# Two-layer decoder trunk: attention norm weights folded into the rows of the output weights, rotary tables made earlier

## The chip, the cores and the metric

The kernel runs on one core of a Trainium2 chip. The metric is the device time of one execution in microseconds, as the median of several runs. The core has five engines that run beside each other, each with its own queue of instructions, which it takes in order: TensorE (PE in the profile; its weight loads are PEld), VectorE (DVE), ScalarE (ACT), GpSimd (POOL), and SyncE (SP), which here only issues DMA transfers (SPq). They wait for one another by semaphores.

## The reference

A decoder trunk of two layers on 256 tokens of width 1024. Layer 0 mixes tokens by gated linear attention (GLA, 4 heads, key width 128, value width 256, chunks of 64), layer 1 by a block-sparse softmax attention with partial rotary embedding; each is followed by a normalisation and a SwiGLU feed-forward. What the change touches:

```python
def gla_mixer(x, w_in, w_gk, b_gk, norm_g, w_out):
    q, k, v, g, gk_low = split_cols(x @ w_in, GLA_COLS)
    ...
    o = from_heads(rms_norm(o.astype(x.dtype), norm_g)) * jax.nn.silu(g)
    return o @ w_out

def partial_rope(x, positions):
    ang = positions.astype(jnp.float32)[:, None, :, None] * inv_freq
    cos, sin = jnp.cos(ang), jnp.sin(ang)
    ...
```

`norm_g` has 256 entries, one for each value feature of a head; the four heads share it. `partial_rope` is used in layer 1 alone, and its tables depend on the positions only.

## The kernel before

All products are done in three matmuls of rounded fp32: a matrix is split into a high part (rounded) and a low part (what is left), and high x high, low x high and high x low are added in PSUM. For weights this is `split`: one DMA of 512 KB into a raw tile (name with `r`), a cast on ScalarE (name with `h`), a subtraction on VectorE (name with `l`). The 256 tokens are two tiles of 128, `t` = 0 and 1.

The order of the first attention as written: `v` block 0, the gate `gk` and from it `z`, `la`, `cum` and three exponentials `em`, `ee`, `ep`; the keys (`wk`, giving `ka`, `ke`, and by copies on GpSimd `kb` and `kx`), the queries (`wq`, giving `qd` in two halves), the scores `sc` and `scx`, `v` block 1 (`wv1`). Then for each token tile the output `o`, the sums of squares `ss`, the two halves of the gate `sg` (weights `wg0`, `wg1`; matmuls, silu on ScalarE, and a multiplication by `normg` on GpSimd), `og` = `o` x `ss` x `sg` on VectorE, its transposes `trg` on TensorE and the split of these into `ogT`. `out_proj` multiplies `ogT` by eight row blocks `wo0` to `wo7` of the output weights into `y`, and adds and normalises. After it `rope_tables` makes the cosine and sine tables of layer 1: three small loads (`rcol`, `cmask`, `posb`), eighteen small VectorE instructions on 32x256 tiles (`ang`, `kk`, `rr`), two sines on ScalarE. The feed-forward (`fg`, `fu`, `A`, `X`, `d`) follows.

No order of instructions is written out. `Plan.op` records each operation with its engine, an assumed duration, what it reads and writes; `Plan.emit` then simulates the engines with these durations and at each step takes the operation that can start first, by order of recording where two can start at once, and before that those marked urgent. The instructions go to the queues in the order so found. Weights and intermediates take 41 slots of SBUF in turn; a load is issued when its slot is free. The planner may therefore put work of a later stage into an earlier one: in the queue of VectorE the rotary instructions stand between the `og` of tile 1 before the change.

Each load on SP also waits for the transfer eight loads back.

Of the kernel before, what the change touches and what calls it, by code (L numbers as in the profile page):

```python
# [10 lines left out]
I32 = mybir.dt.int32  # L11
AF = mybir.ActivationFunctionType
ALU = mybir.AluOpType
# [176 lines left out]
def kernel(ctx, tc, x, positions, gla_w_in, gla_w_gk, gla_b_gk, gla_norm_g, gla_w_out,  # L190
# [30 lines left out]
    normg = fixed("normg", (P, GLA_DV))  # L221
# [29 lines left out]
    def split(name, parts, zero=False):  # L251
# [9 lines left out]
        act(1024, lambda: nc.scalar.copy(hi.r, raw.f), [raw], [hi])  # L261
        dve(1024, lambda: nc.vector.tensor_tensor(out=lo.r, in0=raw.f, in1=hi.f, op=ALU.subtract), [raw, hi], [lo])
# [19 lines left out]
    def w_row(name, w, k):  # L282
        return split(name, lambda raw: [(raw, w[k * P:(k + 1) * P, :])])
# [133 lines left out]
    def out_proj(aT, w, xo, gb, dstT, keep):  # L417
        ws = [w_row(f"wo{k}", w, k) for k in range(KT)]
# [379 lines left out]
    dma(lambda: nc.sync.dma_start(normg.f, gla_norm_g[0:1, :].broadcast_to([P, GLA_DV])), 128, [], [normg])  # L798
# [25 lines left out]

    wv1 = load_cols("wv1", w0, V0 + 512)
# [6 lines left out]
    def g_block(blk, t, ws):  # L832
        ps = pl.buf("acc", f"g{blk}{t}")
        act_block(ps, T0, ws, t)
        sl = slice(512 * blk, 512 * blk + 512)
        act(512, lambda: nc.scalar.activation(sg[t].f[:, sl], ps.f, AF.Silu), [ps], [(sg[t], blk)], table="silu")

        def fg():
            v3 = sg[t].f[:, sl].rearrange("p (j c) -> p j c", j=2)
            nc.gpsimd.tensor_tensor(out=v3, in0=v3, in1=normg.f.unsqueeze(1).broadcast_to([P, 2, GLA_DV]), op=ALU.mult)  # L840
        gps(512, fg, [(sg[t], blk), normg], [(sg[t], blk)])
# [62 lines left out]
    xs = out_proj(ogT, gla_w_out[0], xs, gb, T1, x32)  # L904


    posb, ang, kk_, rr_ = S_("posb"), S_("ang"), S_("kk"), S_("rr")

    def q32(b):
        return b.f[0:ROPE, 0:S]  # L910

    def rope_tables():
        dma(lambda: nc.sync.dma_start(rcol.f, c_f32[:, 2 * P:2 * P + 2]), 4, [], [rcol])
        dma(lambda: nc.sync.dma_start(cmask.f, c_f32[:, P:2 * P]), 64, [], [cmask])
        dma(lambda: nc.sync.dma_start(q32(posb).bitcast(I32), positions[0:1, :].broadcast_to([ROPE, S])), 32,
            [], [posb])

        def f0():
            nc.vector.tensor_copy(q32(ang), q32(posb).bitcast(I32))
            nc.vector.tensor_scalar_mul(q32(ang), q32(ang), rcol.f[0:ROPE, 0:1])  # L920
        dve(512, f0, [posb, rcol], [ang])
        for which, off in ((0, 0.25), (1, 0.0)):
            def f1(off=off, which=which):
                k_, r_, a_ = q32(kk_), q32(rr_), q32(ang)
                nc.vector.tensor_scalar(out=k_, in0=a_, scalar1=1.0 / TWO_PI, scalar2=off, op0=ALU.mult, op1=ALU.add)
                nc.vector.tensor_scalar_add(k_, k_, MAGIC)
                nc.vector.tensor_scalar_add(k_, k_, -MAGIC)
                nc.vector.scalar_tensor_tensor(out=r_, in0=k_, scalar=-C1, in1=a_, op0=ALU.mult, op1=ALU.add)

            def f2(which=which):  # L930
                k_, r_ = q32(kk_), q32(rr_)
                nc.vector.scalar_tensor_tensor(out=r_, in0=k_, scalar=-C2, in1=r_, op0=ALU.mult, op1=ALU.add)
                nc.vector.scalar_tensor_tensor(out=r_, in0=k_, scalar=-C3, in1=r_, op0=ALU.mult, op1=ALU.add)
                if which == 0:
                    nc.vector.tensor_scalar_add(r_, r_, math.pi / 2.0)
# [169 lines left out]
```

## Time and profile before

| | |
|---|---|
| median of 3 runs | 593.11 us (593.08 to 593.64) |
| profiled execution | 594.05 us; its span, first to last instruction, 592.1 us |
| TensorE busy | 578.4 us, 98% of the span |
| VectorE busy | 491.1 us, 83% |
| ScalarE busy | 327.4 us, 55% |
| GpSimd busy | 23.2 us, 4% |
| TensorE's share of the chain that ended last | 86% (VectorE 9%) |
| mean granted clock of TensorE | 0.993 |

Busy shares are means over stages. The waits of an engine say where it stood still and for whom; the timeline then gives the instructions around one wait, with the idle time ahead of an instruction and what ended it in brackets. The profile also has, for any stretch, the share of TensorE's full clock that the chip granted.

### The profile page before, as it was taken

To read this page: it belongs to the slowest core of one execution; us is meant where nothing else is said; L and a number is where in the kernel's file an instruction comes from. 1 tells how busy PE (TensorE), PEld (TensorE's weight loads), DVE (VectorE), ACT (ScalarE), POOL (GpSimd) and SP (SyncE) were. 2 spreads that over 40 slices of the span, in tenths; PEclk is the share of its full clock that TensorE was granted. 3 is DMA by queue.
4 is the path that set the end of the run, shared out by engine and by line. 5 is a ranking of instruction groups with operands and counts; after the bars stand their busy time and mean duration, and the time that the engine had idled before them with its cause. 6 is when DMAs were issued, how large, how long until landed. Compare 5 with 4: busy or idle time off the path is not lost.

```text
span 592.1 us, 8004 instructions
## 1 busy us (share of the span) xinstructions
PE 578.4 (98%) x3030; PEld 494.0 (83%) x3030; DVE 491.1 (83%) x609; ACT 327.4 (55%) x434; POOL 23.2 (4%) x27
## 2 busy tenths in 40 slices
PE   8999998999999999999999999999999999999994
PEld 7899886888888788889888999888888888888883
DVE  5889268889999986999696589988999998689626
ACT  4794455246767634786264356644685775359310
POOL 1022210000000000000000000000000000000001
PEclk9999998999999999999999999999999999999998
DMA  8984285254656737688365435726457484559101
GB/s 285 380 283 150 68 280 184 54 195 163 230 176 201 258 111 215 200 296 277 114 214 181 150 134 192 234 73 213 143 193 234 143 277 150 167 176 311 58 1 71
DMA packets 51880, 110.04 MB, mean 186 GB/s; under 512 B 4689, under 2 KB 9329, under 8 KB 51842
## 3 DMA queue, kind: packets, MB, share of 16 engines
q1 hardware_dynamic: 51842, 109.53, 56.6%
q8 instruction: 24, 0.39, 0.3%
q14 instruction: 14, 0.11, 0.1%
HBM read 108.47 MB, written 1.05 MB: 185 GB/s over the span
## 4 chain that ended last, share of the span: by engine, by line
PE 86%; DVE 9%; issue 2%; DMA 2%; ACT 0%; SPq 0%; DVEq 0%
PE fy L291 6%; PE fy L289 6%; PE fy L290 6%; PE pa L542 3%; PE pa L539 3%; PE pa L541 3%; PE pg L289 3%; PE v L291 3%; PE pg L291 3%; PE v L289 2%; PE v L290 2%; PE pu L289 2%; PE pu L291 2%; PE pg L290 2%; PE pu L290 2%; PE tr L304 2%
## 5 line engine op out<-in xcount | busy, mean ns | idle before, releaser
L559 DVE TENSOR_TENSOR A<-A,X 128x1024 f32<-128x1024 f32 x36 | 43.2, 1218 | 3.3 <-DMA X<-in_ffn_w_gu 3.2
L313 ACT CAST xT<-tr 128x512 fp32r<-128x512 f32 x16 | 9.3, 592 | 40.4 <-PE tr L304 40.4
L360 POOL TENSOR_TENSOR st<-st,mhalf 128x1 f32<-128x1 f32 x8 | 7.5, 944 | 483.6 <-DVE st L358 483.6
L317 DVE TENSOR_TENSOR xT<-tr,xT 128x512 fp32r<-128x512 f32 x16 | 10.7, 686 | 7.7 <-ACT xT L313 5.6
L348 DVE SCALAR_TENSOR_TENSOR r<-xn,fy 128x512 f32<-128x512 f32 x8 | 5.5, 685 | 10.9 <-PE fy L291 10.9
L559 DVE TENSOR_TENSOR X<-X,X 128x1024 f32<-128x1024 f32 x12 | 14.3, 1216 | 0.0
L313 ACT CAST hT3h<-tr 128x512 fp32r<-128x512 f32 x4 | 2.4, 588 | 18.0 <-PE tr L304 18.0
L352 DVE BATCH_NORM_STATS2 st<-r 128x6 f32<-128x512 f32 x16 | 11.1, 693 | 0.5
L370 DVE SCALAR_TENSOR_TENSOR xn<-r,st,lnb 128x512 f32<-128x512 f32 x16 | 11.3, 745 | 0.0
L366 DVE SCALAR_TENSOR_TENSOR r<-r,st,lng 128x512 f32<-128x512 f32 x16 | 11.2, 743 | 0.0
L497 ACT CAST D0h<-A 128x1024 fp32r<-128x1024 f32 x6 | 6.3, 1054 | 8.0 <-DVE A L559 7.9
L497 ACT CAST B0h<-A 128x1024 fp32r<-128x1024 f32 x6 | 6.3, 1052 | 5.8 <-DVE A L559 5.8
L518 DVE TENSOR_TENSOR sil<-pu,sil 128x512 f32<-128x512 f32 x8 | 5.5, 685 | 4.7 <-PE pu L291 4.7
L497 ACT CAST F0h<-X 128x1024 fp32r<-128x1024 f32 x6 | 6.3, 1051 | 5.4 <-DVE X L559 5.4
L497 ACT CAST A0h<-A 128x1024 fp32r<-128x1024 f32 x6 | 6.3, 1046 | 5.0 <-DMA A<-in_ffn_w_gu 5.0
L498 DVE TENSOR_TENSOR C1l<-X,C1h 128x1024 fp32r<-128x1024 f32 x6 | 7.3, 1220 | 1.7 <-ACT C1h L497 1.7
L968 ACT ACTIVATE mk<-mk 128x512 f32<-128x512 f32 x4 | 2.4, 599 | 11.5 <-PE mk L291 11.5
L317 DVE TENSOR_TENSOR hT3l<-tr,hT3h 128x512 fp32r<-128x512 f32 x4 | 2.8, 690 | 7.0 <-ACT hT3h L313 7.0
L498 DVE TENSOR_TENSOR G0l<-A,G0h 128x1024 fp32r<-128x1024 f32 x6 | 7.3, 1217 | 1.5 <-ACT G0h L497 1.5
L304 PE MATMUL tr<-ident,e 128*128 128x128 f32 x48 | 7.3, 274 | 1.1 <-DVE e L586 1.1
L304 PEld LDWEIGHTS tr<-ident,e 128*128 128x128 f32 x48 | 5.7, 140 | 3.0 <-issue 1.8
L497 ACT CAST G0h<-A 128x1024 fp32r<-128x1024 f32 x6 | 6.3, 1048 | 3.2 <-DVE A L559 3.2
(1098 smaller groups left out, 2292.3 us busy)
## 6 DMA issues: line engine op xcount, KB each, us to landing
X<-in_ffn_w_gu SPq DMA_DIRECT2D x36, 512.0 KB, 4.6
A<-in_ffn_w_gu SPq DMA_DIRECT2D x12, 512.0 KB, 4.6
lng<-in_ln_g SPq DMA_DIRECT2D x4, 512.0 KB, 3.9
lnb<-in_ln_b SPq DMA_DIRECT2D x4, 512.0 KB, 5.5
x<-in_x SPq DMA_DIRECT2D x4, 256.0 KB, 4.5
fg00r<-in_ffn_w_gu SPq DMA_DIRECT2D x2, 512.0 KB, 6.1
fg01r<-in_ffn_w_gu SPq DMA_DIRECT2D x2, 512.0 KB, 6.4
fg02r<-in_ffn_w_gu SPq DMA_DIRECT2D x2, 512.0 KB, 5.8
```

What stands on the lines that cost most here:

```text
L289: nc.tensor.matmul(ps, lh, rh, start=start, stop=False)
L290: nc.tensor.matmul(ps, ll, rh, start=False, stop=False)
L291: nc.tensor.matmul(ps, lh, rl, start=False, stop=stop)
L304: nc.tensor.transpose(ps.f[:, j * P:(j + 1) * P], src.f[:, k * P:(k + 1) * P], ident.f)
L313: nc.scalar.copy(view(0), ps.f.rearrange("p (k c) -> p k c", k=4))
L317: nc.vector.tensor_tensor(out=l, in0=ps.f.rearrange("p (k c) -> p k c", k=4), in1=h.bitcast(F32), op=ALU.subtract)
L497: act(1024, lambda: nc.scalar.copy(hi.r, raw.f), [raw], [hi])
L498: dve(1024, lambda: nc.vector.tensor_tensor(out=lo.r, in0=raw.f, in1=hi.f, op=ALU.subtract), [raw, hi], [lo])
L539: nc.tensor.matmul(ps.f, sh, wh.r[:, cs], start=first and q == 0 and j == 0, stop=False, skip_group_check=True)
L541: nc.tensor.matmul(ps.f, sl_, wh.r[:, cs], start=False, stop=False, skip_group_check=True)
L542: nc.tensor.matmul(ps.f, sh, wl.r[:, cs], start=False, stop=last_ and q == 1 and j == 1, skip_group_check=True)
L559: dve(1024, lambda q=q, other=other: nc.vector.tensor_tensor(out=raws[q].f, in0=raws[q].f, in1=other.f, op=ALU.add), [raws[q], other], [ra ...
```

## The change

The multiplication of the gate by `normg` on GpSimd goes. Since `norm_g` multiplies the columns of what `out_proj` multiplies by the output weights, it can as well multiply the rows of these weights: row `p` of block `k` by `norm_g[(k % 2) * 128 + p]`. `normg` becomes a tile of 128x2, loaded by 256 pieces of 4 bytes in place of 128 rows of 1 KB, and `split` gets a scale: the cast becomes an activation (copy) with a scale for each row, the subtraction a `scalar_tensor_tensor` that multiplies the raw weights by the same scale and subtracts the high part. This holds for the eight `wo` of the first attention; the second attention's stay as they are.

`rope_tables` is recorded after the scores, ahead of `v` block 1, instead of ahead of the feed-forward; its text is the same. The planner does the rest.

```diff
--- before.py
+++ after.py
@@ -218,7 +218,7 @@
     cmask = fixed("cmask", (P, P))
     imask = fixed("imask", (P, P), I32)
     rcol = fixed("rcol", (P, 2))
-    normg = fixed("normg", (P, GLA_DV))
+    normg = fixed("normg", (P, GLA_DV // P))
     wgk = fixed("wgk", (GLA_RANK + 1, 512))
     gkT = fixed("gkT", (GLA_RANK + 1, S))
     rope = fixed("rope", (ROPE, 2, S))
@@ -248,7 +248,8 @@
         return pl.op("POOL", 1.3, fn, reads, writes, extra=8.0, **kw)
 
 
-    def split(name, parts, zero=False):
+    def split(name, parts, zero=False, scale=None):
+
         raw, hi, lo = S_(name + "r"), S_(name + "h", True), S_(name + "l", True)
         if zero:
             gps(500, lambda: nc.gpsimd.memset(raw.f, 0.0), [], [raw])
@@ -258,8 +259,13 @@
             for dst, src in parts(raw.f):
                 nc.sync.dma_start(dst, src)
         dma(load, kb, [], [raw])
-        act(1024, lambda: nc.scalar.copy(hi.r, raw.f), [raw], [hi])
-        dve(1024, lambda: nc.vector.tensor_tensor(out=lo.r, in0=raw.f, in1=hi.f, op=ALU.subtract), [raw, hi], [lo])
+        if scale is None:
+            act(1024, lambda: nc.scalar.copy(hi.r, raw.f), [raw], [hi])
+            dve(1024, lambda: nc.vector.tensor_tensor(out=lo.r, in0=raw.f, in1=hi.f, op=ALU.subtract), [raw, hi], [lo])
+        else:
+            act(1024, lambda: nc.scalar.activation(hi.r, raw.f, AF.Copy, scale=scale[1]), [raw, scale[0]], [hi])
+            dve(1024, lambda: nc.vector.scalar_tensor_tensor(out=lo.r, in0=raw.f, scalar=scale[1], in1=hi.f,
+                                                             op0=ALU.mult, op1=ALU.subtract), [raw, hi, scale[0]], [lo])
         return hi, lo
 
     def split2(name, w, k0, c0):
@@ -279,8 +285,8 @@
         src = w[k0 * P:(k0 + nk) * P, c0:c0 + n].rearrange("(k p) c -> p k c", p=P)
         return split(name, lambda raw: [(raw.rearrange("p (k c) -> p k c", k=nk), src)])
 
-    def w_row(name, w, k):
-        return split(name, lambda raw: [(raw, w[k * P:(k + 1) * P, :])])
+    def w_row(name, w, k, scale=None):
+        return split(name, lambda raw: [(raw, w[k * P:(k + 1) * P, :])], scale=scale)
 
     def load_cols(name, w, c0):
         return [w_kcols(f"{name}{i}", w, 2 * i, 2, c0, 512) for i in range(KT // 2)]
@@ -414,8 +420,8 @@
         sl = slice(512 * blk, 512 * blk + 512)
         act(512, lambda: nc.scalar.copy(vt[t].f[:, sl], ps.f), [ps], [(vt[t], blk)])
 
-    def out_proj(aT, w, xo, gb, dstT, keep):
-        ws = [w_row(f"wo{k}", w, k) for k in range(KT)]
+    def out_proj(aT, w, xo, gb, dstT, keep, scale=None):
+        ws = [w_row(f"wo{k}", w, k, scale and scale(k)) for k in range(KT)]
         xn = []
         for t in range(2):
             y = [pl.buf("acc", f"y{t}{hf}") for hf in range(2)]
@@ -795,7 +801,8 @@
     gps(350, lambda: nc.gpsimd.tensor_copy(kxv()[:, 1, :, 0:CHUNK], ch(qd, 2)), [qd], [(kx, 3)])
 
     dma(lambda: nc.sync.dma_start(imask.f, c_i32), 64, [], [imask])
-    dma(lambda: nc.sync.dma_start(normg.f, gla_norm_g[0:1, :].broadcast_to([P, GLA_DV])), 128, [], [normg])
+    dma(lambda: nc.sync.dma_start(normg.f, gla_norm_g[0].rearrange("(c p) -> p c", p=P),
+                                  ), 8, [], [normg])
     scs = [S_("sc0"), S_("scx")]
 
     def scv(i):
@@ -822,6 +829,45 @@
     pe(4 * 512, fscx, [kx], [psx])
     act(512, lambda: nc.scalar.copy(scv(2), psx.f.rearrange("p (h c) -> p h c", h=GLA_H)), [psx], [(scs[1], 0)])
 
+
+    posb, ang, kk_, rr_ = S_("posb"), S_("ang"), S_("kk"), S_("rr")
+
+    def q32(b):
+        return b.f[0:ROPE, 0:S]
+
+    def rope_tables():
+        dma(lambda: nc.sync.dma_start(rcol.f, c_f32[:, 2 * P:2 * P + 2]), 4, [], [rcol])
+        dma(lambda: nc.sync.dma_start(cmask.f, c_f32[:, P:2 * P]), 64, [], [cmask])
+        dma(lambda: nc.sync.dma_start(q32(posb).bitcast(I32), positions[0:1, :].broadcast_to([ROPE, S])), 32,
+            [], [posb])
+
+        def f0():
+            nc.vector.tensor_copy(q32(ang), q32(posb).bitcast(I32))
+            nc.vector.tensor_scalar_mul(q32(ang), q32(ang), rcol.f[0:ROPE, 0:1])
+        dve(512, f0, [posb, rcol], [ang])
+        for which, off in ((0, 0.25), (1, 0.0)):
+            def f1(off=off, which=which):
+                k_, r_, a_ = q32(kk_), q32(rr_), q32(ang)
+                nc.vector.tensor_scalar(out=k_, in0=a_, scalar1=1.0 / TWO_PI, scalar2=off, op0=ALU.mult, op1=ALU.add)
+                nc.vector.tensor_scalar_add(k_, k_, MAGIC)
+                nc.vector.tensor_scalar_add(k_, k_, -MAGIC)
+                nc.vector.scalar_tensor_tensor(out=r_, in0=k_, scalar=-C1, in1=a_, op0=ALU.mult, op1=ALU.add)
+
+            def f2(which=which):
+                k_, r_ = q32(kk_), q32(rr_)
+                nc.vector.scalar_tensor_tensor(out=r_, in0=k_, scalar=-C2, in1=r_, op0=ALU.mult, op1=ALU.add)
+                nc.vector.scalar_tensor_tensor(out=r_, in0=k_, scalar=-C3, in1=r_, op0=ALU.mult, op1=ALU.add)
+                if which == 0:
+                    nc.vector.tensor_scalar_add(r_, r_, math.pi / 2.0)
+                nc.vector.tensor_scalar(out=r_, in0=r_, scalar1=SIN_MAX, scalar2=-SIN_MAX, op0=ALU.min, op1=ALU.max)
+            dve(900, f1, [ang], [kk_, rr_])
+            dve(900, f2, [kk_, rr_], [rr_])
+            act(256, lambda which=which: nc.scalar.activation(rope.f[:, which, :], q32(rr_), AF.Sin), [rr_],
+                [(rope, which)], table="silu")
+        dve(256, lambda: nc.vector.tensor_scalar_mul(rope.f[:, 1, :], rope.f[:, 1, :], rcol.f[0:ROPE, 1:2]),
+            [(rope, 1), rcol], [(rope, 1)])
+
+    rope_tables()
     wv1 = load_cols("wv1", w0, V0 + 512)
     v_block(1, 0, T0, wv1, v_sb)
 
@@ -834,11 +880,6 @@
         act_block(ps, T0, ws, t)
         sl = slice(512 * blk, 512 * blk + 512)
         act(512, lambda: nc.scalar.activation(sg[t].f[:, sl], ps.f, AF.Silu), [ps], [(sg[t], blk)], table="silu")
-
-        def fg():
-            v3 = sg[t].f[:, sl].rearrange("p (j c) -> p j c", j=2)
-            nc.gpsimd.tensor_tensor(out=v3, in0=v3, in1=normg.f.unsqueeze(1).broadcast_to([P, 2, GLA_DV]), op=ALU.mult)
-        gps(512, fg, [(sg[t], blk), normg], [(sg[t], blk)])
 
     wgs = [load_cols("wg0", w0, G0), load_cols("wg1", w0, G0 + 512)]
     for t in range(2):
@@ -901,49 +942,10 @@
     gb = load_ln(0, 0)
     T1 = new_xT("xT1")
     x32 = [S_("x32a"), S_("x32b")]
-    xs = out_proj(ogT, gla_w_out[0], xs, gb, T1, x32)
-
-
...
     gb = load_ln(0, 1)
     T2 = new_xT("xT2")
-    rope_tables()
     xs = ffn(0, xs, T1, gb, T2, False, x32)
 
 
```

(The removed copy of `rope_tables` is left out; it reads as the added one.)

Where it lands. VectorE at the end of the first attention, before (`og` is that of tile 1, `ss` its scale by the sums of squares; `kk` and `rr` are rotary):

```order
L936 TENSOR_SCALAR rr_894<-rr_894 32x256
L262 TENSOR_TENSOR fg00l_932<-fg00r_885,fg00h_907 128x1024
L925 TENSOR_SCALAR kk_893<-ang_889 32x256
L926 TENSOR_SCALAR kk_893<-kk_893 32x256
L927 TENSOR_SCALAR kk_893<-kk_893 32x256
L928 SCALAR_TENSOR_TENSOR rr_894<-kk_893,ang_889 32x256
L262 TENSOR_TENSOR fg01l_953<-fg01r_905,fg01h_922 128x1024
L896 TENSOR_TENSOR ogT_763<-trg_943,ogT_762 128x512
L879 SCALAR_TENSOR_TENSOR og_0_909<-o_0_822,ss_829,sg_0_887 128x256 x2
L932 SCALAR_TENSOR_TENSOR rr_894<-kk_893,rr_894 32x256
L933 SCALAR_TENSOR_TENSOR rr_894<-kk_893,rr_894 32x256
L936 TENSOR_SCALAR rr_894<-rr_894 32x256
```

and after:

```order
L920 SCALAR_TENSOR_TENSOR og_0_912<-o_0_833,ss_852,sg_0_910 128x256 x2
L264 TENSOR_TENSOR fg00l_931<-fg00r_893,fg00h_923 128x1024
L264 TENSOR_TENSOR fg01l_943<-fg01r_908,fg01h_935 128x1024
L264 TENSOR_TENSOR fg02l_959<-fg02r_920,fg02h_947 128x1024
L920 SCALAR_TENSOR_TENSOR og_0_912<-o_0_845,ss_852,sg_0_910 128x256
L937 TENSOR_TENSOR ogT_787<-trg_949,ogT_786 128x512
L920 SCALAR_TENSOR_TENSOR og_0_912<-o_0_845,ss_852,sg_0_910 128x256
L264 TENSOR_TENSOR fg03l_981<-fg03r_933,fg03h_965 128x1024
```

The rotary instructions are gone from between the parts of `og`; the splits of `fg01` and `fg02` have come ahead of the second half of `og`, which is now taken in two steps.

ScalarE at the same place, before:

```order
L836 ACTIVATE sg_0_887<-g_0_837 128x512
L261 CAST fg00h_907<-fg00r_885 128x1024
L261 CAST fg01h_922<-fg01r_905 128x1024
L939 ACTIVATE rope<-rr_894 32x256
L261 CAST fg02h_935<-fg02r_930 128x1024
L836 ACTIVATE sg_0_887<-g_0_878 128x512
L892 CAST ogT_762<-trg_943 128x512
```

and after:

```order
L882 ACTIVATE sg_0_910<-g_0_860 128x512
L263 CAST fg00h_923<-fg00r_893 128x1024
L263 CAST fg01h_935<-fg01r_908 128x1024
L263 CAST fg02h_947<-fg02r_920 128x1024
L882 ACTIVATE sg_0_910<-g_0_901 128x512
L933 CAST ogT_786<-trg_949 128x512
```

The sine ahead of `fg02h` is gone; the second silu still stands behind the cast of `fg02h`.

VectorE in the front of the first attention, before (`z`, `cum`, `ee` lead to the exponentials):

```order
L733 TENSOR_SCALAR z_311<-pre_308 128x512
L262 TENSOR_TENSOR wq2l_333<-wq2r_242,wq2h_299 128x1024
L742 TENSOR_TENSOR z_311<-z_311,la_313 128x1024
L744 SCALAR_TENSOR_TENSOR cum_395<-smask_90,z_311 128x1024
L753 TENSOR_TENSOR ee_411<-cum_395 128x1024
L262 TENSOR_TENSOR wq3l_429<-wq3r_273,wq3h_376 128x1024
L262 TENSOR_TENSOR wv10l_444<-wv10r_296,wv10h_393 128x1024
```

and after:

```order
L264 TENSOR_TENSOR wq2l_333<-wq2r_242,wq2h_301 128x1024
L845 CAST ang_349<-posb_298 32x256
L846 TENSOR_SCALAR ang_349<-ang_349,rcol 32x256
L851 TENSOR_SCALAR kk_352<-ang_349 32x256
L852 TENSOR_SCALAR kk_352<-kk_352 32x256
L853 TENSOR_SCALAR kk_352<-kk_352 32x256
L854 SCALAR_TENSOR_TENSOR rr_353<-kk_352,ang_349 32x256
L858 SCALAR_TENSOR_TENSOR rr_353<-kk_352,rr_353 32x256
L859 SCALAR_TENSOR_TENSOR rr_353<-kk_352,rr_353 32x256
L861 TENSOR_SCALAR rr_353<-rr_353 32x256
L862 TENSOR_SCALAR rr_353<-rr_353 32x256
L748 TENSOR_TENSOR z_313<-z_313,la_315 128x1024
```

Ten rotary instructions stand between the split of `wq2` and `z`. The second pass stands further on, among `ka`, `ke` and `kx`, and on ScalarE a table load and a sine stand ahead of the exponentials, a second pair behind the casts of `wv1`; the casts of `wv10` and `wv11` have moved behind the exponentials. On SP `rcol`, `cmask` and `posb` are issued right behind `normg`, ahead of `wv10r`. On TensorE two things move: the six matmuls of `wv11` for `v` of tile 0 go ahead of the scores, and the second `trg` of tile 0 goes ahead by six matmuls.

## Rows read from the trace of the kernel before

**Rows 1.** Waits of TensorE over the whole span: us in total, times, longest.
```profile
PE trg L888 <- DVE og L879: 2.7, 1, 2.7
...
PE tr L304 <- DVE e L586: 1.1, 1, 1.1
```

**Rows 2.** Timeline of TensorE: start, length, engine, line, operation, idle before.
```profile
92.14 0.60 PE L888 MATMUL trg<-ident,og 128*128 128x128 f32 x4
...
93.98 0.39 PE L289 MATMUL y<-wo2h,ogT 128*128 128x512 f32 x1
...
98.92 1.08 PE L888 MATMUL trg<-ident,og 128*128 128x128 f32 x4 [2.67 <-DVE og L879]
...
102.30 0.40 PE L289 MATMUL y<-wo7h,ogT 128*128 128x512 f32 x1
```

**Rows 3.** Stretches: busy time of each engine with instructions, PEclk, DMA share, GB/s.
```profile
60.00:80.00 20.00, 20.00 (x94) 16.65 (x93) 8.23 (x12) 10.70 (x21) 3.60 (x3) 1.00 0.39 133
...
98.90:102.30 3.40, 3.38 (x10) 2.84 (x11) 3.02 (x6) 1.83 (x3) 0.00 (x0) 0.51 0.35 69
199.70:204.70 5.00, 4.99 (x24) 4.23 (x25) 5.00 (x6) 4.29 (x5) 0.00 (x0) 1.00 0.73 220
```

**Rows 4.** Timelines of ScalarE, GpSimd and VectorE ahead of that `trg`.
```profile
93.14 0.42 ACT L939 ACTIVATE rope<-rr 32x256 f32<-32x256 f32 x1 [1.76 <-DVE rr L936]
93.47 1.03 ACT L261 CAST fg02h<-fg02r 128x1024 fp32r<-128x1024 f32 x1
94.41 0.59 ACT L836 ACTIVATE sg<-g 128x512 f32<-128x512 f32 x1
...
95.07 1.30 POOL L840 TENSOR_TENSOR sg<-sg,normg 128x512 f32<-128x512 f32 x1 [6.14 <-ACT sg L836]
...
95.19 1.46 DVE L928 SCALAR_TENSOR_TENSOR rr<-kk,ang 32x256 f32<-32x256 f32 x1
...
97.71 0.67 DVE L896 TENSOR_TENSOR ogT<-trg,ogT 128x512 fp32r<-128x512 f32 x1
98.31 0.85 DVE L879 SCALAR_TENSOR_TENSOR og<-o,ss,sg 128x256 f32<-128x256 f32 x2
```

**Rows 5.** Lines of VectorE, 60 to 100 us: busy us, mean ns, idle before.
```profile
L879 DVE SCALAR_TENSOR_TENSOR og<-o,ss,sg 128x256 f32<-128x256 f32 x8 | 3.5, 472 | 5.3 <-POOL sg L840 5.3
```

**Rows 6.** The load of fg02r, by its tile: issue on SP, and landing.
```profile
L259 SPq DMA_DIRECT2D fg02r<-in_ffn_w_gu x1: 368/368/368, 86.7 to 86.7; - x1
...
DMA to landing us min/median/max: 5.0/5.0/5.0
```

**Rows 7.** Timeline of ScalarE, 28 to 32 us: a table load.
```profile
29.60 1.28 ACT L741 ACT_TABLE_LOAD   x1
30.89 1.06 ACT L741 ACTIVATE la<-la 128x1024 f32<-128x1024 f32 x1
```

**Rows 8.** Timeline of VectorE: front of the attention, and the first rotary pass.
```profile
31.98 1.23 DVE L742 TENSOR_TENSOR z<-z,la 128x1024 f32<-128x1024 f32 x1 [3.00 <-ACT la L741]
...
43.12 1.41 DVE L262 TENSOR_TENSOR wv12l<-wv12r,wv12h 128x1024 fp32r<-128x1024 f32 x1
...
50.00 0.68 DVE L773 SCALAR_TENSOR_TENSOR qd<-gq,ep 128x512 f32<-128x512 f32 x1
...
87.76 1.32 DVE L919 CAST ang<-posb 32x256 f32<-32x256 int32 x1 [2.37 <-DMA posb<-in_positions]
89.11 0.34 DVE L920 TENSOR_SCALAR ang<-ang,rcol 32x256 f32<-32x256 f32 x1
...
93.04 1.20 DVE L262 TENSOR_TENSOR fg00l<-fg00r,fg00h 128x1024 fp32r<-128x1024 f32 x1
```

**Rows 9.** The load of wv10r, by its tile: issue on SP, and landing.
```profile
L259 SPq DMA_DIRECT2D wv10r<-in_gla_w_in x1: 379/379/379, 18.0 to 18.0; - x1
...
DMA to landing us min/median/max: 9.8/9.8/9.8
```

**Rows 10.** Timeline of TensorE: the first scores.
```profile
50.14 0.33 PE L811 MATMUL sc<-qd,ka 128*128 128x64 f32 x2
```

More of the change, by code (lines that the diff above doesn't have):

```diff
@@ L903 @@
     x32 = [S_("x32a"), S_("x32b")]
-    xs = out_proj(ogT, gla_w_out[0], xs, gb, T1, x32)
[L907 to L935, printed above, removed]
-                nc.vector.tensor_scalar(out=r_, in0=r_, scalar1=SIN_MAX, scalar2=-SIN_MAX, op0=ALU.min, op1=ALU.max)
-            dve(900, f1, [ang], [kk_, rr_])
-            dve(900, f2, [kk_, rr_], [rr_])
-            act(256, lambda which=which: nc.scalar.activation(rope.f[:, which, :], q32(rr_), AF.Sin), [rr_],
-                [(rope, which)], table="silu")
-        dve(256, lambda: nc.vector.tensor_scalar_mul(rope.f[:, 1, :], rope.f[:, 1, :], rcol.f[0:ROPE, 1:2]),
-            [(rope, 1), rcol], [(rope, 1)])
@@ L944 @@
+    xs = out_proj(ogT, gla_w_out[0], xs, gb, T1, x32, lambda k: (normg, normg.f[:, k % 2:k % 2 + 1]))
     gb = load_ln(0, 1)
     T2 = new_xT("xT2")
-    rope_tables()
     xs = ffn(0, xs, T1, gb, T2, False, x32)
```

## The prediction

> **What bounds the kernel now.** I read the waits of TensorE first. TensorE is busy for 98% of the span, and where it waits it waits for single events: the longest is 2.7 us at the transposes `trg` of the first attention, for `og` of VectorE; the next that lies inside the work is 1.1 us in the first feed-forward [rows 1]. So what the change is worth is read at that one `trg`. The timeline of TensorE there shows two costs. It sat idle for 2.67 us before the second `trg` of token tile 1, and then ran slowly: from that `trg` to the first matmul of `wo7` 3.38 us passed (98.92 to 102.30), where the same set of work, the first `trg` of that tile with seven matmuls, took 1.84 us (92.14 to 93.98) [rows 2]. The granted clock says why: 0.51 in that stretch, about 1.2 GHz, after an idle stretch, and 1.00 (2.4 GHz) in the stretch behind the 1.13 us wait in the feed-forward [rows 3]. So this wait cost 2.67 + 1.54 = 4.2 us, and an idle of 1.1 us costs only itself.
>
> Then the chain ahead of it, by the timeline of the other engines. The silu of `sg` (the second half of the gate) started at 94.41, though the last gate matmul was over by about 92.3 (the `trg` behind it started at 92.14): ScalarE, which takes its work in order, had waited 1.76 us for the rotary `rr` and then run a sine and a cast [rows 4]. GpSimd multiplied the gate by `normg` from 95.07 to 96.37. VectorE, in order too, was meanwhile in a rotary `rr` that took 1.46 us, then split `fg01l`, then did `ogT`, and came to `og` at 98.31 [rows 4]. Each of these three delays is taken away or moved by the change.
>
> **The change part by part.** *The multiplication on GpSimd goes.* Four instructions of 1.3 us, two of which VectorE waited for (5.3 us) [rows 5]. For tile 0 TensorE had other work; for tile 1 this is a link of the chain above.
>
> *Rotary work leaves the tail.* In the new order of VectorE three weight splits stand between the two halves of `og`, then `og`, `ogT`, `og`; ScalarE has the cast `fg02h` and then the silu. What is late next is the load of `fg02r`: it was issued at 86.7 and landed 5.0 us later, at 91.7 [rows 6]; I take no earlier landing. The cast starts there, the silu 0.94 us behind it (93.47 to 94.41 in [rows 4]), at about 92.65, later than the matmuls' end. VectorE splits `fg02l` from about 92.8 to 93.95 (a split starts 1.14 us after the one ahead of it, as `ogT` at 97.71 would follow `fg01l` at 96.57 [rows 4]); two `og` of 0.4 us (half of the pair's 0.85 [rows 4]) and an `ogT` of 0.6 between them end at about 95.3. TensorE needs it at 98.92 - 2.67 = 96.25 [rows 2]. That leaves 0.9 us, so the wait goes, and the slow stretch with it: **-4.2 us**. If a gap of a microsecond stays, it costs just that.
>
> *The weights are scaled while they are split.* The eight `wo` casts become activations with a scale per row. The activation of the same size took 1.06 us, a cast 1.03 [rows 4, 7]. The eight subtractions get a scalar operand; the nearest row with one is `og`, 0.47 us for 256 columns [rows 5], which bounds 1024 columns by 1.9 us where a split takes 1.20 [rows 8]: up to 0.7 us each, 5 us in eight. The low bound is nothing, since the reads are the same in number, and I take it: the 0.47 holds the cost of starting four times. Cover: VectorE was busy for only 8.2 of the 20 us from 60 to 80, where most of them lie [rows 3].
>
> *Rotary tables come early.* Their ten VectorE instructions of the first pass now stand in front of `z`, where VectorE had been idle for 3.00 us [rows 8]. In the trace of before the pass runs from 87.76 to 93.04, with an `og` pair inside it: 5.28 - 0.85 = 4.4 us. But its first instruction, the cast of the positions, took 1.32 us and the following one on the same 32x256 tile 0.34 [rows 8], while GpSimd was at work on `sg`. With 0.34 for the cast too the pass takes 3.45 us. So `z` comes 0.45 us later (1.4 us if the cast really is that long). I take the shorter, as there is no GpSimd work at that place; both stay in the range. The Trainium skill says in "SBUF — State Buffer", section "Who interferes with whom", that VectorE and GpSimd share a port pair as an exclusive lock, and that the second to come blocks. By that rule the early cast is short, and the sum is the one taken here; by the row alone it would be 1 us worse on VectorE.
>
> The positions must have landed by then. Their load takes its turn just ahead of `wv10r`, behind the transfers that stood ahead of `wv10r` before and two small ones (66 KB). `wv10r` was issued at 18.0 and landed 9.8 us later, at 27.8 [rows 9]; VectorE is free at 28.98 (31.98 - 3.00, [rows 8]). The four small loads push `wv10r` to `wv12r` back, but these are split from 44 us on.
>
> The second pass has neither cast nor first multiplication nor one of the additions: 2.6 us, and 0.3 for the last multiplication. Against this two fewer splits stand ahead of the second half of `qd`: -2.3 us. So `qd`, which started at 50.00 [rows 8], starts at 50.0 + 0.45 + 2.9 - 2.3 = 51.05 and ends by 51.8. TensorE now does six more matmuls of `v` (1.4 us) ahead of the scores `sc`, which started at 50.14 [rows 10], and needs this half only for heads 2 and 3, 0.85 us later: at 52.4. Margin 0.6 us, so **0 us** here; with the long cast 0.4 us of waiting, and with copies of GpSimd in between some more (`wv12l`, next to such copies, took 1.41 instead of 1.20 [rows 8]; five copies by 0.2 are 1.0 us).
>
> ScalarE gets a table load and a sine (1.28 + 0.42 = 1.7 us [rows 4, 7]) in place of two casts (1.9 us) ahead of the exponentials: nothing. A second pair falls into a stretch where it then idles.
>
> *Behind the attention* TensorE has no wait but the 1.1 us [rows 1], and loads and splits there follow its progress, so the 4.2 us last to the end.
>
> **The rivals.** *The tail is still late:* `fg02r` lands later than 91.7, since the loads ahead of it fight for the same queue. Above 0.9 us of lateness each microsecond costs one; 2 us later leaves a gap of 1.1 us without a slow stretch: 590.0. For it: ScalarE waits in order for this cast; against: the loads are issued no later than before. The long cast or the copies of GpSimd in front cost up to 1 us: 589.9.
>
> *A table load costs more than its row.* If each of the first two loads drew 1.4 us behind it, the exponentials would come 2.8 us later, less the 0.65 us of hold that `z` and the casts leave, and `qd` 2.1 us later: 1.5 us of waiting, 590.4. Against it: the load starts at 29.60, lasts 1.28, and the logarithm starts at 30.89 [rows 7]. The Trainium skill, "ScalarE: Activation LUTs", section "What ACT_TABLE_LOAD costs", adds a drain of about 1.38 us to each switch; the trace does not agree here.
>
> *Slower:* VectorE and GpSimd stop each other in front. The second rotary pass stands among GpSimd's five copies of `kb` and `kx`. If each held VectorE as the multiplication of `sg` held the `rr` of 1.46 us [rows 4], by 1.1 us, `qd` would come 5.5 us later, less 0.6 us of margin: 4.9 us of waiting before `sc`, and 1.5 for the slow clock behind it, 6.4 against 4.2: 595.3. It decides from a delay of 3.3 us on. Against it: the 0.2 us that `wv12l` lost.
>
> *It does nothing:* `og` of tile 1 waits for something else just as long, and the gap stays: 593.1.
>
> **How the numbers follow.** The profiled execution took 594.05 us, 1.95 more than its span; the median of three runs is 593.11, 0.94 lower. I take the saving off the median: 593.11 - 4.2 = 588.9. Chances: forecast 0.72 (588.3 to 589.6; the runs of before spread over 0.56), late tail or front up to 1 us 0.15, table loads 0.04, slower 0.04, nothing 0.05. The range goes from 588.3, the forecast less that spread, to 590.5, which takes in the first two rivals. A measurement of this kernel tells about 0.2% (1.2 us) from no change. Faster by more than that: 0.91; within it 0.05; slower 0.04.
>
> **What would show it.** After: no wait of `trg` for `og` above 1 us, a granted clock of 1.00 around 95 to 105, silu of the last `sg` near 92.7, `og` right behind `fg02l`; in front `z` near 32.4, the early cast near 0.3 us, no wait at `sc`. Wrong if TensorE waits at `sc` for `qd`, or at `trg` with `fg02h` late, or if a new wait in the feed-forward swallows the lead.

## The result, and the profile of the changed kernel

The changed kernel takes 588.86 us (median of 6 runs, 588.54 to 589.37), the kernel before, run beside it, 593.29 us: a ratio of 0.9935, 95% interval 0.9922 to 0.9948. That is faster by 4.4 us, or 0.65%. Two repeats on other occasions gave 0.9928 (0.9914 to 0.9943) and 0.9932 (0.9920 to 0.9944). The profiled execution took 588.95 us, with a span of 587.1 us.

The waits of TensorE in the changed kernel (us in total, times, longest), beside [rows 1]; these two stand at the start of the program, and the waits for `og` and for `e` are gone:

```profile
PE tr L310 <- DMA x<-in_x: 1.4, 2, 0.9
PE junk L668 <- DVE zeros L661: 1.1, 1, 1.1
```

The timeline of TensorE, beside [rows 2], and the stretch of [rows 3]:

```profile
92.45 0.60 PE L929 MATMUL trg<-ident,og 128*128 128x128 f32 x4
...
96.39 0.60 PE L929 MATMUL trg<-ident,og 128*128 128x128 f32 x4
96.75 0.48 PE L295 MATMUL y<-wo5h,ogT 128*128 128x512 f32 x1
...
98.22 0.40 PE L295 MATMUL y<-wo7h,ogT 128*128 128x512 f32 x1
```

```profile
98.90:102.30 3.40, 3.40 (x16) 2.74 (x15) 2.50 (x3) 0.61 (x1) 0.00 (x0) 1.00 0.53 154
```

No bracket stands behind the second `trg`, so there was no idle time. From it to `wo7h` 1.83 us passed, where before it was 3.38, and the clock is 1.00, the 2.4 GHz level. The six matmuls from 96.75 to 98.22 start about 0.24 us apart, though each is recorded for 0.39 or more: the next one starts before the recorded end of the last.

The saving is in one place. The table cuts the profiled executions at four events of TensorE's timeline: the first `trg` of token tile 1, the first matmul of the feed-forward (`fg00h`), the first matmul of layer 1 (`mv00h`) and the last matmul.

| us | to first `trg` | `trg` to `fg00h` | `fg00h` to `mv00h` | `mv00h` to the end |
|---|---|---|---|---|
| before | 92.14 | 28.53 | 180.06 | 283.89 |
| after | 92.45 | 24.16 | 178.99 | 284.01 |
| difference | +0.31 | -4.37 | -1.07 | +0.12 |

The 1.07 us are the wait for `e` [rows 1]. Two further profiles of the kernel before don't have it (178.7 and 179.0 us in that column), nor has any other kernel below (178.7 to 179.7 us): it belongs to one execution and not to the change. The 0.31 us arise at the start, around the landing of `x`; in the profiles below, but for the one with work added in front, the first `trg` lies anywhere between 91.4 and 92.8 us. In what follows the second column is the measure, since it holds neither.

How the tail came out, on ScalarE and VectorE, beside [rows 4]:

```profile
92.31 1.05 ACT L263 CAST fg02h<-fg02r 128x1024 fp32r<-128x1024 f32 x1 [0.33 <-DMA fg02r<-in_ffn_w_gu]
93.26 0.59 ACT L882 ACTIVATE sg<-g 128x512 f32<-128x512 f32 x1
...
93.39 1.23 DVE L264 TENSOR_TENSOR fg02l<-fg02r,fg02h 128x1024 fp32r<-128x1024 f32 x1
94.53 0.48 DVE L920 SCALAR_TENSOR_TENSOR og<-o,ss,sg 128x256 f32<-128x256 f32 x1
94.92 0.68 DVE L937 TENSOR_TENSOR ogT<-trg,ogT 128x512 fp32r<-128x512 f32 x1
95.52 0.47 DVE L920 SCALAR_TENSOR_TENSOR og<-o,ss,sg 128x256 f32<-128x256 f32 x1
```

`og` follows `fg02l` without a break, with one `ogT` between its halves, and is over at 95.99, 0.40 us before TensorE comes to `trg`. In the two repeats that margin was 0.22 and 0.20 us.

The front, beside [rows 7, 8, 10]:

```profile
29.21 0.28 DVE L845 CAST ang<-posb 32x256 f32<-32x256 int32 x1
...
32.72 1.21 DVE L748 TENSOR_TENSOR z<-z,la 128x1024 f32<-128x1024 f32 x1
...
33.22 1.28 ACT L865 ACT_TABLE_LOAD   x1
34.51 0.42 ACT L865 ACTIVATE rope<-rr 32x256 f32<-32x256 f32 x1
...
50.54 0.67 DVE L779 SCALAR_TENSOR_TENSOR qd<-gq,ep 128x512 f32<-128x512 f32 x1
```

And the two halves of one of the eight scaled splits, one on each engine (busy us, mean ns, idle before):

```profile
L266 ACT ACTIVATE wo0h<-wo0r,normg 128x1024 fp32r<-128x1024 f32 x1 | 1.2, 1155 | 0.0
L267 DVE SCALAR_TENSOR_TENSOR wo0l<-wo0r,normg,wo0h 128x1024 fp32r<-128x1024 f32 x1 | 1.3, 1283 | 0.1
```

### The profile page after: what moved, and what is told of

It is laid out like the page before. It is cut to its first block, busy times and chain, and to the rows that moved or that the text cites. A ratio compares the mean times of both kernels' runs of the same rounds, so it can differ in the third digit from the quotient of the medians.

```text
span 587.1 us, 7993 instructions
## 1 busy us (share of the span) xinstructions
PE 577.0 (98%) x3030; PEld 493.2 (84%) x3030; DVE 489.2 (83%) x609; ACT 331.4 (56%) x436; POOL 16.5 (3%) x23
## 3 DMA queue, kind: packets, MB, share of 16 engines
HBM read 108.34 MB, written 1.05 MB: 186 GB/s over the span
## 4 chain that ended last, share of the span: by engine, by line
PE 97%; DMA 1%; DVE 1%; SPq 0%; issue 0%; DVEq 0%
PE fy L297 7%; PE fy L295 7%; PE fy L296 7%; PE pa L548 4%; PE pa L545 4%; PE pa L547 4%; PE tr L310 3%; PE v L295 3%; PE v L297 3%; PE pg L297 3%; PE pg L295 3%; PE y L296 3%; PE y L297 3%; PE y L295 3%; PE pg L296 3%; PE v L296 3%
## 5 line engine op out<-in xcount | busy, mean ns | idle before, releaser
L920 DVE SCALAR_TENSOR_TENSOR og<-o,ss,sg 128x256 f32<-128x256 f32 x8 | 3.6, 479 | 8.7 <-ACT sg L882 8.7
L503 ACT CAST C1h<-X 128x1024 fp32r<-128x1024 f32 x6 | 6.3, 1052 | 3.4 <-DMA X<-in_ffn_w_gu 2.1
L503 ACT CAST D1h<-A 128x1024 fp32r<-128x1024 f32 x6 | 6.3, 1056 | 3.2 <-DVE A L565 2.9
```

## The experiments

The theory: the whole gain is the idle time at the second `trg` of token tile 1 and the stretch of slow clock behind it. The questions were which part of the change takes it away, how much room is left, and whether the two prices (idle time, clock) are what the prediction said. The times are medians of several runs, but for two kernels that were run once, for their profile. The runs fall into three groups, and the kernel before was run beside each: 593.03 us beside the two parts, the changed kernel again (588.39) and the moved `trg`; 592.52 beside the first two delays and GpSimd's added work, where the changed kernel was not run; 592.88 beside the second run of the rotary part, the changed kernel once more (588.70) and the two single runs.

**The weights scaled alone.** The changed kernel with `rope_tables` at its old place:

```diff
-    rope_tables()
     wv1 = load_cols("wv1", w0, V0 + 512)
...
     T2 = new_xT("xT2")
+    rope_tables()
     xs = ffn(0, xs, T1, gb, T2, False, x32)
```

> The change without its second part: the norm weights scale the rows of wo and nothing is left for GpSimd between silu and og, but the rotary tables are made at the old place, in the tail of the first attention. Theory A (rotary work and GpSimd each delay og by more than half of what is missing, so either one alone takes most of the gap away): the cast of the positions takes 0.3 us instead of 1.32 and no rotary instruction is held to 1.46 us, so the silu of the last sg starts about 1 us earlier (93.4), og follows within 1 us of it, the idle time ahead of the second trg of token tile 1 falls from 2.67 to under 1 us, the clock there is 1.00, and the time is 589.0 to 590.0. Rival B (the rotary work alone is the delay, GpSimd's multiplication is hidden behind it): a gap of 2 us or more stays, clock about 0.5 behind it, time 592 to 593.

Measured: 591.43 us, ratio 0.9979 (0.9958 to 1.0000). By the medians that is 1.6 of 4.6 us, about a third of the gain. In the profiled execution `trg` to `fg00h` took 26.08 us, a bit over half of the gain; it had full clock behind the gap, and the ten runs go from 589.77 to 594.03 us, with mean clocks from 0.998 to 0.993. TensorE, VectorE and ScalarE:

```profile
97.77 0.74 PE L891 MATMUL trg<-ident,og 128*128 128x128 f32 x4 [1.63 <-DVE og L882]
...
89.27 0.28 DVE L922 CAST ang<-posb 32x256 f32<-32x256 int32 x1 [1.84 <-DMA posb<-in_positions]
...
94.67 1.21 DVE L264 TENSOR_TENSOR fg01l<-fg01r,fg01h 128x1024 fp32r<-128x1024 f32 x1
95.80 0.28 DVE L928 TENSOR_SCALAR kk<-ang 32x256 f32<-32x256 f32 x1
...
97.15 0.86 DVE L882 SCALAR_TENSOR_TENSOR og<-o,ss,sg 128x256 f32<-128x256 f32 x2
...
94.90 0.58 ACT L844 ACTIVATE sg<-g 128x512 f32<-128x512 f32 x1
```

The cast took 0.28 us, as theory A expected. But the silu came no sooner (94.90, which is 2.17 us behind the first `trg`, where it was 2.27 before), and the gap stayed at 1.63 us, between the two theories; the expectation of under 1 us failed. The gate was done at 95.5, and `og` started 1.65 us later, because the rest of a split and four rotary instructions stood ahead of it in VectorE's queue. The order costs as much as the gap is long. Part of the gap is TensorE's own order: in this kernel the planner put the second `trg` ahead of the three matmuls of `wo4`, which stand in front of it before and after the change and take 0.7 us. At the old place the gap would have been about 0.9 us (an estimate from these two numbers), so this run shows too little of what the first part alone can bring. The clock behind this gap was 1.00.

**The rotary tables alone**, run on two occasions: the kernel before with `rope_tables` where the change puts it, and GpSimd's multiplication kept.

```diff
+    rope_tables()
     wv1 = load_cols("wv1", w0, V0 + 512)
...
-    rope_tables()
     xs = ffn(0, xs, T1, gb, T2, False, x32)
```

> The change without its first part: the rotary tables are made early, but GpSimd still multiplies the gate by the norm weights, so the kernel splits wo as before. Theory A: the silu of the last sg starts at 92.7 as with the whole change, GpSimd multiplies from 93.3 to 94.6, og starts at 94.7 to 95.3 and both halves are over at 96 to 96.5, against 96.3 when TensorE needs them: a gap of 0 to 1 us, clock 1.00, time 588.9 to 590. Rival C (the multiplication on GpSimd, and what it holds on VectorE, is the delay, the rotary work is hidden): the gap stays at 2 us or more, 592 to 593. In both the early cast of the positions takes 0.3 us, since GpSimd is idle there.

> The rotary tables made early and nothing else, in more rounds beside the whole change. In the first look TensorE came to the second trg of token tile 1 just as og was done: no idle time, but no margin either. Theory A (with the rotary work out of the tail, GpSimd's multiplication only uses up margin): the same time as the whole change within 0.3 us, gap under 0.3 us. Rival (the multiplication still costs): 0.4 to 0.8 us more than the whole change.

Measured: 588.79 us, ratio 0.9937 (0.9919 to 0.9955), and with more runs 589.36 us, 0.9943 (0.9931 to 0.9955). `trg` to `fg00h` took 24.39 and 24.27 us, against 24.15 of the whole change beside it both times. GpSimd, VectorE and TensorE in the second profile:

```profile
94.17 1.84 POOL L879 TENSOR_TENSOR sg<-sg,normg 128x512 f32<-128x512 f32 x1 [4.57 <-ACT sg L875]
...
93.64 1.22 DVE L262 TENSOR_TENSOR fg02l<-fg02r,fg02h 128x1024 fp32r<-128x1024 f32 x1 [0.18 <-ACT fg02h L261]
...
96.05 0.87 DVE L918 SCALAR_TENSOR_TENSOR og<-o,ss,sg 128x256 f32<-128x256 f32 x2 [0.59 <-POOL sg L879]
...
96.71 0.71 PE L927 MATMUL trg<-ident,og 128*128 128x128 f32 x4
```

So the move of the rotary tables brings nearly everything. The multiplication is on the way, since VectorE waits 0.59 us for it, but it eats up margin first and costs 0.1 to 0.2 us in the tail. The medians are 0.40 us apart on the first occasion and 0.66 on the second, which falls into the rival's 0.4 to 0.8, so theory A's 0.3 failed; but the intervals of the two ratios overlap both times, so the size of this difference is not clear of noise. The second pair of profiles puts only 0.12 us of it into the tail: the spans are 0.2 us apart, and what lies around the span is 2.2 us in place of 1.8, in every run of the two kernels on both occasions. Why that is so wasn't tried.

**The changed kernel again**, as the mark:

> The changed kernel again, as it is, beside the three above on the same chip. Both theories: 588.9 (588.5 to 589.4); no wait at the second trg of token tile 1. It serves as the mark for the others, and as a second look at the wait for e in the first feed-forward.

> The changed kernel as it is, in more rounds, as the mark for the one above. Both: 588.2 to 588.9.

Measured: 588.39 us, a little under the range given for it, and 588.70 us; no wait for `og`, none for `e`.

**The kernel before with only the `trg` moved.**

```diff
-            pe(4 * 256, trg, [(og[t], (blk, 0)), (og[t], (blk, 1)), ident], [ps], urgent=True)
+            late = t == 1 and blk == 1
+            pe(4 * 256, trg, [(og[t], (blk, 0)), (og[t], (blk, 1)), ident], [ps], urgent=not late,
+               prio=len(pl.ops) + 45 if late else None)
```

> The kernel before with one thing moved: the second trg of token tile 1 stands on TensorE behind the rest of the matmuls of token tile 0 for the first half of y (some 30 matmuls, 7 us later), and the split into ogT goes with it; all operations are kept, the multiplication on GpSimd and the rotary work in the tail too. Theory A (the whole gain is that gap of 2.67 us and the slow stretch of 1.54 us behind it): no idle time at that trg, clock 1.00 from 95 to 105, time 588.9 to 589.5, the same as the whole change. Rival D (part of the gain comes from elsewhere, from work that is gone or from the wait of 1.1 us in the first feed-forward): half of the gain or less, 590.5 to 592. The wait of 1.1 us for e in the first feed-forward: if it is bound to the change, it is still there; if it varies from execution to execution, it may be gone.

Measured: 590.30 us, ratio 0.9959 (0.9946 to 0.9973); `trg` to `fg00h` 26.01 us: 2.5 us of the 4.4. The gap and the slow clock are gone, but `ogT`, which now stands behind other work on VectorE, is late in its place:

```profile
108.39 0.50 PE L290 MATMUL y<-wo4h,ogT 128*128 128x512 f32 x1 [0.94 <-DVE ogT L898]
...
110.68 1.38 PE L304 MATMUL tr<-ident,xn 128*128 128x128 f32 x8 [0.16 <-DVE xn L370]
```

Of the 1.85 us that are missing, 1.1 are these waits. Each of them costs 0.16 us more than its bracket, which counts from the recorded end of the matmul in front, though the next could have started 0.23 us behind its start. And the eight transposes `tr` took 1.38 us, where they take 1.04 in the changed kernel. That makes 1.76 of the 1.85. The run bears the theory out as far as it goes (all operations kept, 2.5 us gained by one move), but it doesn't show that 4.4 us hang on the gap alone. The two runs that put a delay back do that better.

**A delay put back into the changed kernel.** The last `og` is done several times over, with the same operands:

```diff
+                    for _ in range(4 if (t, blk, j) == (1, 1, 1) else 1):
                         nc.vector.scalar_tensor_tensor(out=og[t].f[:, hs], in0=ob[blk].f[:, j * S:(j + 1) * S],
```

(8 in place of 4 in the second and third.)

> The changed kernel with the last of the four og instructions of token tile 1's second half done four times over into the same place (three more by 0.42 us, 1.25 us of VectorE time), nothing else moved in any queue. In the changed kernel og is over about 0.35 us before TensorE comes to the trg behind it. Theory A (the margin is those 0.35 us, and what is late beyond it goes straight into the time, at full clock): idle time of 0.9 us ahead of that trg, clock 1.00 behind it, time 588.4 + 0.9 = 589.3. Rival E (the lost time is caught up later, since work behind the attention had slack): gap as said, time still 588.4 to 588.7. Rival F (any idle time brings the slow stretch): 589.3 + 1.5 = 590.8.

> The same with the last og done eight times over (seven more by 0.42 us, 2.9 us), nothing else moved. Theory A: idle time of 2.6 us ahead of the trg, like the 2.67 us of the kernel before, and behind it a stretch at about 0.5 of the clock that costs 1.5 us: 588.4 + 2.6 + 1.5 = 592.5; runs spread by more than 1.5 us, as those of the kernel before and of the one with the weights scaled alone do. Rival G (the slow stretch of the kernel before had another cause than the idle time): 591.0, clock 1.00. Rival E (caught up later): under 590.5.

> The kernel with the last og done eight times over, once more, for its profile. In the first profile the idle time of 3.67 us was followed by full clock, while most of its runs were 1 to 3 us longer at a lower mean clock. Theory (the slow stretch behind a long idle time comes in some executions and not in others): about 8 in 10 that this profile shows a clock of about 0.5 for some us behind the gap, with a span 1 to 3 us longer than the 591.0 of the first. Rival (the longer runs lose their time elsewhere): clock 1.00 from 95 to 110 again, whatever the span.

Measured: 590.55 us for four (0.9975, 0.9962 to 0.9988), 594.10 us for eight (1.0031, 1.0015 to 1.0047, slower than the kernel before), 593.94 us for eight in the single run. The second `trg`, and for eight the stretches behind it (TensorE's busy time comes first, the clock is the third number from the end), in the order of the three profiles:

```profile
98.37 0.44 PE L930 MATMUL trg<-ident,og 128*128 128x128 f32 x2 [1.45 <-DVE og L921]
```

```profile
100.21 0.44 PE L930 MATMUL trg<-ident,og 128*128 128x128 f32 x2 [3.67 <-DVE og L921]
...
100.20:102.00 1.80, 1.79 (x9) 1.51 (x10) 1.80 (x2) 1.32 (x2) 0.00 (x0) 1.00 0.00 0
102.00:105.00 3.00, 3.00 (x15) 2.40 (x14) 2.96 (x5) 1.17 (x2) 0.00 (x0) 1.00 0.43 121
```

```profile
100.22 0.44 PE L930 MATMUL trg<-ident,og 128*128 128x128 f32 x2 [3.13 <-DVE og L921]
...
101.20:104.60 3.40, 3.40 (x10) 2.71 (x9) 2.63 (x5) 1.97 (x3) 0.00 (x0) 0.54 0.27 58
```

Each repeat took 0.52 us (four took 2.03, eight 4.11), not the 0.42 assumed, and the margin was 0.1 us or nothing in the first two, 0.5 us in the third (3.63 us of delay, 3.13 of idle time). With that the idle time goes into the time one for one, with 0.2 to 0.3 us on top, and is not made up later: `trg` to `fg00h` is 25.86 us with four (1.71 us over the 24.15 of the changed kernel, for a bracket of 1.45), and everything behind it is as long as before. The 590.55 us of four lie near the 590.8 of the rival F, but not for its reason: the clock behind the gap was 1.00 in the profile, and the repeats were longer than assumed. The rule for the clock was too simple. The same kernel had 3.67 us of idle time and full clock behind it (28.04 us, 3.9 over), and in another execution 3.13 us and a stretch near the 1.2 GHz level (29.04 us, 4.9 over; with the 0.2 us on top of the bracket, about 1.5 for the clock). The ten runs of eight go from 591.73 to 595.88 us.

**The kernel before again**, twice:

> The kernel before again, as it is. Expected of every theory: the gap of 2.5 to 2.8 us at the second trg of token tile 1, time 593.0. Open is whether the wait of 1.1 us for e in the first feed-forward is there again (then it belongs to the kernel before, and the change has taken it away too, since no run without that gap had it) or not (then it varies from execution to execution), and whether the slow stretch behind the gap is.

> The kernel before once more, for its profile. The idle time of 2.7 us at the second trg of token tile 1 is there again; the slow stretch behind it in 6 of 10; no wait of 1.1 us for e in the first feed-forward, as in the second profile of this kernel.

Measured: 592.50 and 591.89 us. `trg` in both, and the stretch behind it in the second:

```profile
98.21 0.80 PE L888 MATMUL trg<-ident,og 128*128 128x128 f32 x4 [2.68 <-DVE og L879]
```

```profile
97.75 1.08 PE L888 MATMUL trg<-ident,og 128*128 128x128 f32 x4 [2.29 <-DVE og L879]
...
97.70:101.00 3.30, 3.25 (x10) 2.76 (x11) 3.03 (x6) 1.83 (x3) 0.00 (x0) 0.51 0.29 65
```

From `trg` to `wo7h` 3.17 and 3.43 us passed, 1.34 and 1.60 more than the 1.83 of the changed kernel; in the first of the two the slow clock goes on behind `wo7h`. By the whole tail, `trg` to `fg00h`, they took 28.67 and 28.19 us. With the 28.53 of the profile that the prediction read, that is three times a price of 4.0 to 4.5 us over the 24.16 of the changed kernel, of which 1.5 to 1.7 us are the clock's.

In the second, GpSimd and VectorE met in the other order:

```profile
94.71 2.37 POOL L840 TENSOR_TENSOR sg<-sg,normg 128x512 f32<-128x512 f32 x1 [6.57 <-ACT sg L836]
...
97.11 0.88 DVE L879 SCALAR_TENSOR_TENSOR og<-o,ss,sg 128x256 f32<-128x256 f32 x2 [0.57 <-POOL sg L840]
```

The rotary `rr` of 1.46 us [rows 4] took 0.42 here, the multiplication of the gate 2.37 in place of 1.30, and `og` waited 0.57 us for it. So in one execution of three the multiplication was the last link of the chain, and the gap was 2.29 us all the same.

**GpSimd beside the early cast.** Four multiplications are put on GpSimd in the front of the changed kernel:

```diff
+    scr = fixed("scr", (P, 256))
...
+    def fscr():
+        for i in range(4):
+            nc.gpsimd.tensor_tensor(out=scr.f, in0=z.f[:, 256 * i:256 * i + 256], in1=z.f[:, 0:256], op=ALU.mult)
+    pl.op("POOL", 0.05, fscr, [z], [scr])
```

> The changed kernel with four GpSimd multiplications of 128x256 added in front: they read z and write a scratch tile that nobody reads, and start when the second z is done (28.2 us), so that they run beside the split of wq2, the cast of the positions and the next rotary instructions on VectorE; no instruction of another engine is moved. GpSimd takes 0.65 us for each, 2.6 us in all. Theory A (what GpSimd multiplies holds the cast, as it held the cast of 1.32 us in the tail): the cast takes up to 0.9 us more than its 0.28, or instructions next to it do, z comes 1 to 2.5 us later than the 32.7 us of the changed kernel; the scores sc, which have 0.5 us of margin, wait 0.5 to 2 us, time 588.9 to 590.4. Rival H (the cast of 1.32 us in the tail was long for another reason): no VectorE instruction there is longer by more than 0.1 us, z at 32.7, time 588.4.

Measured: 589.42 us, ratio 0.9956 (0.9942 to 0.9970). GpSimd and VectorE:

```profile
27.46 4.12 POOL L743 TENSOR_TENSOR scr<-z 128x256 f32<-128x256 f32 x4 [24.71 <-DVE z L740]
...
29.29 0.82 DVE L850 CAST ang<-posb 32x256 f32<-32x256 int32 x1
30.15 0.77 DVE L851 TENSOR_SCALAR ang<-ang,rcol 32x256 f32<-32x256 f32 x1
30.95 0.77 DVE L856 TENSOR_SCALAR kk<-ang 32x256 f32<-32x256 f32 x1
31.76 0.28 DVE L857 TENSOR_SCALAR kk<-kk 32x256 f32<-32x256 f32 x1
...
34.26 1.21 DVE L753 TENSOR_TENSOR z<-z,la 128x1024 f32<-128x1024 f32 x1
```

Three instructions were held by 0.54, 0.43 and 0.49 us, and the next, after GpSimd's last, had its 0.28 again: `z` came 1.54 us later. With the 0.28 us that the cast took at its old place once the multiplication was gone (above), the 1.32 us of [rows 8] were a wait for GpSimd, and the rival falls. What such a delay of `z` costs the kernel stays open: no wait appeared at `sc`, but TensorE was itself 1.57 us late in that execution, by a stretch of low clock in the front (below).

The margin in the tail was used up here:

```profile
98.70 0.44 PE L934 MATMUL trg<-ident,og 128*128 128x128 f32 x2 [0.35 <-DVE og L925]
```

The cast of `fg02h` started 0.94 us behind the first `trg`; in the changed kernel it started 0.14 us ahead of it.

## Why the prediction was right, and where its steps were off

- **The price of the gap.** 2.67 + 1.54 = 4.2 us was put on it; the tail of the first attention got 4.37 us shorter, and the median went from 593.11 in the first runs to 588.86, where 588.9 was predicted. The missing 0.17 us are a misreading. The 2.67 us count from the recorded end of the matmul in front of the gap (96.25), but that matmul started at 95.85, and the next could have started 0.23 us later, at 96.08; so the gap cost 2.84 us, and 2.84 + 1.54 = 4.38. (Six matmuls, not seven, stand between the `trg` and the end of that stretch; they do so on both sides.) The idle time is a firm price. The 1.54 us is one of several values that this stretch can have, nothing among them; that it lies at 1.5 to 1.7 in all three profiles of the kernel before is why it held. That the median came within 0.1 us is luck: the three medians of the changed kernel are 588.39, 588.70 and 588.86.
- **The tail's timetable** was right in its chain and too generous in its margin. With the 0.31 us of late start taken off, silu came at 92.95 (predicted 92.65), `og` ended at 95.68 (95.3), and TensorE came at 96.08 (96.25, the misreading above): 0.4 us of room, not 0.9, and 0.2 in the repeats. Of the 0.5 us, 0.3 are the load of `fg02r`. The prediction took its landing of before, 91.7 [rows 6], as the worst. It was issued 2.2 us earlier than before and landed no earlier, since it now took 7.7 us:

```profile
L260 SPq DMA_DIRECT2D fg02r<-in_ffn_w_gu x1: 367/367/367, 84.5 to 84.5; - x1
...
DMA to landing us min/median/max: 7.7/7.7/7.7
```

The casts of `fg00`, `fg01` and `fg02` each waited for their load, at 89.66, 90.92 and 92.31, so these loads landed one behind another; what would bring them sooner was not tried. The rival of the late tail, which had a chance of 0.15, was 0.2 to 0.4 us away from coming true, and in the kernel with GpSimd's added work it did, with a wait of 0.35 us.

- **Which part does it.** The prediction gave each of three delays a share. The runs put nearly all on the rotary work, by its place in two queues. With the rotary work gone, GpSimd's multiplication costs 0.1 to 0.2 us in the tail; with it in place, it was the last link in one of three executions.
- **Scaled splits at nothing:** right. The subtractions take 1.28 us in place of 1.22, 0.06 more where the bound was 0.7, and the activations 1.15 in place of 1.05. VectorE was busy for 10.1 of the 20 us from 60 to 80, 8.2 before [rows 3], and TensorE waited for none of it.
- **The front.** `z` was predicted near 32.4 and came at 32.72, which is 32.41 with the late start off; the cast took 0.28 us. The second half of `qd` came earlier than thought, at 50.54 and not 51.05, and its margin at `sc` was about 1.4 us in place of 0.6. The mis-sized term is the copies of GpSimd: they now run earlier, beside three of the rotary instructions, which they lengthen by 0.1 us each, and no longer beside `wv12l` and its two neighbours, which had lost 0.2 us each.
- **Table loads.** The sine started 1.29 us after the load, with no further gap, as the logarithm did [rows 7], so this rival's 1.4 us didn't come. The Trainium skill, "ScalarE: Activation LUTs", section "What ACT_TABLE_LOAD costs", has a drain of about 1.38 us on top of each load; no row here shows it.
- **VectorE and GpSimd stopping each other in front:** the mechanism exists, as the four added multiplications show, but the copies were short. The rival's 1.1 us for each was too much for them.

## What to carry to other kernels

When the bounding engine waits once, read the queues of the engines that feed it: here some of eighteen small instructions of a later stage, recorded late and scheduled early, stood ahead of the one that was needed, and moving them to a place with idle time gained nearly all, while the more visible hand-over to GpSimd was mostly hidden behind them. Two delays that lie side by side don't add: the parts alone gained 1.6 and 4.2 us, both together 4.6 (medians of the first group), though in the first of them TensorE's order differed too. And look at the margin that is left, not only at the wait that is gone: here it is 0.2 to 0.4 us, set by one load.

## What the hardware showed that was not expected

**The clock after idle time is not a fixed price.** About the same idle time was followed by full clock in one execution and by a stretch near the lower level in another (3.67 and 3.13 us idle above). Of the other gaps, 1.45 and 1.63 us were followed by full clock, 2.29, 2.67 and 2.68 by the slow stretch. Where it came, it cost 1.5 to 1.7 us. And in the kernel with GpSimd's added work the clock fell in the front, behind an idle time of only 0.27 us and the short matmuls `pre` on 17 rows:

```profile
25.53 1.99 PE L735 MATMUL pre<-gkT,wgk 17*128 17x256 f32 x8 [0.27 <-DVE gkT L727]
...
28.00:32.00 4.00, 4.00 (x23) 4.00 (x22) 3.90 (x6) 3.73 (x5) 3.35 (x4) 0.57 0.94 334
```

In the changed kernel the same 4 us have 35 matmuls at 1.00; here there are 23, and from the start of `pre` to the first matmul of `wq0` 13.58 us passed in place of 12.09. What made it fall stays open: in the single run with eight `og` TensorE was idle for 0.31 us ahead of the same `pre`, and these 4 us had 36 matmuls at 1.00. The Trainium skill, "TensorE: Matmul & The Clock Gate", "Part 1: The HAM clock gate", says of the start of a kernel that the number of slow matmuls differs between runs of one kernel; the runs here show the like in the middle of a program.

**GpSimd is held as much as it holds.** The multiplication of `sg` took 1.30 us in the kernel before [rows 4] and 1.84 beside the split `fg02l`, and the copy of `kx` from `qd`, 1.33 us before, took 2.80 in the changed kernel beside splits. These splits kept their 1.2 us, where `wv12l` beside the copies of the kernel before had taken 1.41 [rows 8]. The Trainium skill, "SBUF — State Buffer", section "Who interferes with whom", gives the rule that the first to issue keeps the shared port for its whole instruction and the other blocks; these rows agree with it.

**The same instruction into the same place** costs 0.52 us a time, where the second `og` of a pair, into another place, adds 0.4 to the 0.48 of the first. Why was not tried.
